# Convolution stages spread through the attention, and the maximum pass traced earlier

## The chip, the cores and the metric

The kernel runs on one core of a Trainium2 chip. The metric is the device time of one execution in microseconds, as the median of several runs. TensorE (PE) multiplies matrices, VectorE (DVE), ScalarE (ACT) and GpSimd (POOL) do the rest, and SyncE (SP) issues most DMAs. Each engine takes its instructions in order from its own queue and waits on semaphores.

## What is computed

The reference is one layer of a hybrid encoder over 2048 tokens of width 1024, in float32. Cut to what matters here:

```python
proj = u @ w_in
a  = mla_group(q part, kv part)          # 8 heads: softmax(q k^T * scale) v over 2048 keys
hy = hyena_group(conv part, filters)     # two orders; 512 channels
#   for o in 0, 1:  y = irfft(rfft(z, 4096) * filt_f[o])[:2048];  z = gate[o] * (y + z * bias[o])
mixed = concat(rms_norm(a), rms_norm(hy)) @ w_o
x = layer_norm(alpha * x + gate * mixed)
...                                      # then 16 routed experts, each choosing 256 tokens
```

The attention and the two long convolutions need only the projections. They don't depend on each other until `w_o` joins them.

## The kernel before

The program is traced in Python. A planner then puts each engine's instructions in order: it runs down the program on a simulated clock and gives a free engine the earliest traced instruction that is ready by that clock. So the traced order is a priority, and the order in which the chip works is fixed before it runs.

**The attention** (`attention`, L771) takes 32 blocks, each of one head and 512 queries. A block `n` has 16 inner steps `k` of 128 keys each. A step makes the scores in a PSUM bank `s` with three matmuls (L866 to L868: high and low halves of the numbers), takes two exponentials of them on ScalarE (`eh` L874 and the full one L875), the low half `el` on VectorE (L65), adds `eh` to the row sums `acc` on POOL (L881), and two steps later multiplies with the values (`pv`, L859 and L860, into the banks `o` and `l`). The exponentials need each query's maximum. It is found a block ahead: 16 times `max_step` (L798), a matmul into a bank `x` and a reduction on VectorE (L805). Then `max_row` (L807) takes the maximum of four parts, copies it into column 96 of `mz` (L811), transposes `mz` on TensorE (L814) and writes the row into the queries (L815), where the next block's first score reads it. `max_row` is traced at step 14. `close_block` (L825) ends the block before at step 3, and stores its output from SP's queue (L837).

**The convolutions** (`hyena`, L631) are a generator that works through stages of each order `o`, on channel halves `i`: `spectrum` (8 tasks), `fwd1` (8 tasks, the first transform), the middle stages `first_half` and `second_half` (16 tasks of each: transform, product with the spectrum on VectorE, ScalarE and POOL, transform back), and `inv` (8 tasks). Between stages the data goes through DRAM (Ad, F_dr, Bd, Z1). A task issues its loads and its stores itself, all from SP's queue, in the order in which they are traced. All its matmuls use one PSUM bank, `h` (`psH`, L931). Loads land in the tags `ta` (three buffers), `tb` and `tc` (two each).

**Side by side.** `beside` (L917) first makes values and keys of the later heads, then runs `hyena`. `drive` (L945 and L946) takes 1.5 of its steps for each of the first 12 steps of the attention, and 0.7 for each later one; what is left comes behind the attention (L947). Then `w_o` follows (weights from L984 on, output of the attention and the convolutions from L991 on).

Of the kernel before, what the change touches and what calls it, by code (L numbers as in the profile page):

```python
# [48 lines left out]
def hybrid_layer(ctx, tc, I, out):  # L49
# [581 lines left out]
    def hyena(hp, hw, bk):  # L631
# [7 lines left out]

        def fwd1(o, i, q4):  # L640
            hc = slice(i * HC, (i + 1) * HC)
            w1c = hw.tile([128, 4, 256], F32, name="ta", bufs=3)
            SY.dma_start(w1c, I["k_w1c"][:, q4 * 1024:q4 * 1024 + 1024].rearrange("p (q m) -> p q m", q=4))
            zt = hw.tile([128, 4, HC], F32, name="tb")
            SY.dma_start(zt, ZS[o][:, q4 * 4:q4 * 4 + 4, hc])
            for q2 in range(2):
                ev = hw.tile([128, 2, 2, HC], F32, name="tc")
                for qq in range(2):
                    ql = q2 * 2 + qq
                    p = bk("h")  # L650
                    for mt in range(2):
                        T.matmul(p[:, mt * HC:(mt + 1) * HC], w1c[:, ql, mt * 128:mt * 128 + 128], zt[:, ql, :],
                                 start=True, stop=True)
                    A.activation(ev[:, :, qq, :], p.rearrange("p (m c) -> p m c", m=2), AF.Copy)
                    if qq == 0:
                        yield
                for mt in range(2):
                    q0 = q4 * 4 + q2 * 2
                    SY.dma_start(Ad[2 * o + i][mt * 128:mt * 128 + 128, q0:q0 + 2, :], ev[:, mt])
                yield  # L660

        def spectrum(o, g4):
            kt = hw.tile([128, 4, CH], F32, name="tc")
            SY.dma_start(kt, pat(Af[o], g4 * 4 * 128 * CH, [[CH, 128], [128 * CH, 4], [1, CH]]))
            for g2 in range(2):
                ev = hw.tile([128, 2, CH], F32, name="ta", bufs=3)
                for gg in range(2):
                    p = bk("h")
                    T.matmul(p, g2m[:, 1 if g4 + g2 + gg == 0 else 0, :], kt[:, g2 * 2 + gg, :], start=True, stop=True)  # L669
                    A.activation(ev[:, gg, :], p, AF.Copy)  # L670
                    if gg == 0:
                        yield
                g0 = g4 * 4 + g2 * 2
                SY.dma_start(F_dr[o][g0:g0 + 2].rearrange("g p c -> p g c"), ev)
                yield

        def first_half(o, i, g4):
            hc = slice(i * HC, (i + 1) * HC)
            kt = hw.tile([128, 4, HC], F32, name="ta", bufs=3)
            SY.dma_start(kt, pat(Ad[2 * o + i], g4 * 4 * 128 * HC, [[HC, 128], [128 * HC, 4], [1, HC]]))  # L680
            ff = hw.tile([128, 4, 2, HC], F32, name="tc")
            for hh in range(2):
                SY.dma_start(ff[hh * 64:hh * 64 + 64], pat(F_dr[o], g4 * 4 * 128 * CH + i * HC,
                                                           [[CH, 64], [128 * CH, 4], [64 * CH, 2], [1, HC]]))
            ys = YS[g4] = []
            for g2 in range(2):
                gs = slice(g2 * 2, g2 * 2 + 2)
                p = bk("h")
                for gg in range(2):
                    gi = g2 * 2 + gg  # L690
                    T.matmul(p[:, gg * HC:(gg + 1) * HC], zm[:, 2 if g4 + gi == 0 else 0, :], kt[:, gi, :],
                             start=True, stop=True)
                pv = p.rearrange("p (g c) -> p g c", g=2)
                pr = hw.tile([128, 2, HC], F32, name="pr")
                V.tensor_tensor(pr, pv, ff[:, gs, 0], OP.mult)
                zs = hw.tile([128, 2, HC], F32, name="zs")
                A.activation(zs[0:64], pv[64:128], AF.Copy, scale=-1.0)
                A.activation(zs[64:128], pv[0:64], AF.Copy)
                yield
                if g4 + g2 == 0:  # L700
                    p = bk("h")
                    T.matmul(p[:, 0:HC], zm[:, 3, :], kt[:, 0, :], start=True, stop=True)
                    A.activation(zs[:, 0], p[:, 0:HC], AF.Copy)
                G.tensor_tensor(zs, zs, ff[:, gs, 1], OP.mult)
                y = hw.tile([128, 2, HC], F32, name="y", bufs=4)
                G.tensor_tensor(y, pr, zs, OP.add)
                ys += [y[:, 0], y[:, 1]]

        def second_half(o, i, g4):
            bt = hw.tile([128, 4, HC], F32, name="tb")  # L710
            ys = YS.pop(g4)
            for g2 in range(2):
                pi = bk("h")
                for gg in range(2):
                    gi = g2 * 2 + gg
                    T.matmul(pi[:, gg * HC:(gg + 1) * HC], ivm[:, 1 if g4 == 0 and gi == 0 else 0, :], ys[gi],  # L716
                             start=True, stop=True)
                A.activation(bt[:, g2 * 2:g2 * 2 + 2, :], pi.rearrange("p (g c) -> p g c", g=2), AF.Copy)
                yield
            SY.dma_start(pat(Bd[2 * o + i], g4 * 4 * 128 * HC, [[HC, 128], [128 * HC, 4], [1, HC]]), bt)  # L720

        def inv(o, i, q4):
# [4 lines left out]
            gt = hw.tile([128, 4, HC], F32, name="tb")  # L727
            SY.dma_start(gt, HZ[1 + o][:, qs, hc])
            for q2 in range(2):
                b2 = hw.tile([128, 2, 2, HC], F32, name="tc")  # L730
                q0 = q4 * 4 + q2 * 2
                SY.dma_start(b2, Bd[2 * o + i][:, q0:q0 + 2, :].rearrange("(k p) q c -> p k q c", k=2))
                p = bk("h")
                for qq in range(2):
                    for kt in range(2):
                        T.matmul(p[:, qq * HC:(qq + 1) * HC], w2i[:, q2 * 2 + qq, kt, :], b2[:, kt, qq, :],
                                 start=kt == 0, stop=kt == 1)
                q_ = slice(q2 * 2, q2 * 2 + 2)
                V.tensor_tensor(gt[:, q_], p.rearrange("p (q c) -> p q c", q=2), gt[:, q_], OP.mult)
                if q2 == 0:  # L740
                    yield
            SY.dma_start(ZO[o][:, qs, hc], gt)

        YS = {}

        def turns(*gens):
            gens = list(gens)
            while gens:
                for g in list(gens):
                    if next(g, gens) is gens:  # L750
                        gens.remove(g)
                    else:
                        yield

        for o in range(2):
            for g4 in range(8):
                yield from spectrum(o, g4)
            for i in range(2):
                for q4 in range(4):
                    yield from fwd1(o, i, q4)  # L760
            for i in range(2):
                yield from first_half(o, i, 0)
                for g4 in range(1, 9):
                    yield from turns(second_half(o, i, g4 - 1), *([first_half(o, i, g4)] if g4 < 8 else []))
            for i in range(2):
                for q4 in range(4):
                    yield from inv(o, i, q4)
                    yield
# [927 lines left out]
```

## Time and profile before

| | us |
|---|---|
| median of 3 runs | 3455.32 (3454.94 to 3457.93) |
| the profiled execution | 3456.35 |
| its span in the trace | 3454.6 |
| blocks of the attention, first score to last close | 661 to 1872 |
| first dense matmuls of the next stage | about 1957 |
| mean granted TensorE clock | 0.958 of full speed |

All rows below come from one profiled execution. Times are microseconds unless marked ns. Busy time of TensorE is the time in which at least one matmul was under way. "PEclk" is the granted clock as a share of 2.4 GHz. A line such as `A <- B: 29.9, 15, 5.3` says that A's engine stood idle before A until B came: 29.9 us in total, 15 times, 5.3 at the longest.

### The profile page before, as it was taken

How to read it: one execution, taken by the hardware profiler on the slowest of the kernel's cores; microseconds unless marked ns; L12 is line 12 of the kernel's file. 1: busy time of each engine (PE TensorE's matmuls, PEld its weight loads, DVE VectorE, ACT ScalarE, POOL GpSimd, SP SyncE). 2: the span in 40 equal slices, each digit the busy share in tenths (PEclk: the TensorE clock that was granted, in tenths of full speed). 3: DMA queues.
4: the chain of work that ended last, by engine and by line, in shares of the span. 5: the costliest groups of instructions: out<-in, count | busy, mean ns of one | idle time of the engine just before them, and what ended most of it. 6: DMA issues, size and time to landing. Idle time of an engine off the chain costs nothing.

```text
span 3454.6 us, 41964 instructions
## 1 busy us (share of the span) xinstructions
PE 3196.6 (93%) x14790; PEld 2477.7 (72%) x14790; DVE 2301.5 (67%) x3528; ACT 1697.8 (49%) x2569; POOL 1456.5 (42%) x1134
## 2 busy tenths in 40 slices
PE   7899999899989999999998699599999999999897
PEld 3667787666767776677776488477788877887676
DVE  7975343776677776667774377776656566565886
ACT  4762222566667664667774244233444344444442
POOL 5750000556678784658886266300100010000564
PEclk9999999699999999999999899799999999999998
DMA  6444353356466467647456643455666566665784
GB/s 192 158 150 118 111 145 94 97 175 175 156 162 150 108 160 236 176 165 163 119 126 194 222 155 131 150 171 186 215 199 203 183 217 210 208 203 186 268 279 160
DMA packets 373755, 594.16 MB, mean 172 GB/s; under 512 B 36859, under 2 KB 190013, under 8 KB 373097
## 3 DMA queue, kind: packets, MB, share of 16 engines
q1 hardware_dynamic: 347097, 528.95, 48.5%
q0 software_dynamic: 26304, 62.00, 7.1%
q8 instruction: 117, 1.92, 0.2%
q14 instruction: 93, 0.76, 0.1%
q10 hardware_dynamic: 144, 0.52, 0.0%
HBM read 438.84 MB, written 152.58 MB: 171 GB/s over the span
## 4 chain that ended last, share of the span: by engine, by line
PE 70%; DVE 11%; DMA 8%; issue 4%; POOL 3%; ACT 3%; SPq 0%; POOLq 0%; DVEq 0%; ACTq 0%
PE g L73 9%; PE g L74 9%; PE g L75 8%; PE s L866 3%; PE s L867 3%; PE s L868 3%; PE o L859 3%; PE l L860 3%; PE x L803 3%; PE mm L75 3%; PE mm L74 3%; PE mm L73 3%; DMA w<-in_w_ada_dram 3%; PE h L669 2%; PE h L716 1%
## 5 line engine op out<-in xcount | busy, mean ns | idle before, releaser
L881 POOL TENSOR_TENSOR acc<-acc,eh 128x512 f32<-128x512 f32 x480 | 615.8, 1283 | 157.3 <-ACT eh L874 132.3
L65 DVE TENSOR_TENSOR wl<-raw,wh 128x2048 fp32r<-128x2048 f32 (+1 forms) x210 | 473.3, 2256 | 225.0 <-ACT wh L59 224.0
L59 ACT ACTIVATE wh<-raw 128x2048 fp32r<-128x2048 f32 x192 | 367.5, 1915 | 439.9 <-PE g L75 341.4
L65 DVE TENSOR_TENSOR el<-s,eh 128x512 fp32r<-128x512 f32 x512 | 349.2, 687 | 158.2 <-ACT s L875 153.2
L805 DVE TENSOR_REDUCE mx<-x 128x1 f32<-128x512 f32 x512 | 346.4, 685 | 140.5 <-PE x L803 138.1
L73 PE MATMUL g<-wh,xh 128*128 128x512 f32 x1024 | 411.1, 402 | 3.2 <-DVE xh L62 2.3
L74 PE MATMUL g<-wl,xh 128*128 128x512 f32 x1024 | 408.3, 399 | 1.6 <-DVE wl L65 1.5
L75 PE MATMUL g<-wh,xl 128*128 128x512 f32 x1024 | 407.5, 398 | 1.0 <-DVE xl L65 1.0
L874 ACT ACTIVATE eh<-s 128x512 fp32r<-128x512 f32 x512 | 304.9, 596 | 205.1 <-PE s L868 179.0
L1495 POOL DMA_INDIRECT ACC<-ye,idx x30 | 65.8, 2195 | 691.0 <-DVE ye L1486 565.5
L875 ACT ACTIVATE s<-s 128x512 f32<-128x512 f32 x512 | 304.5, 595 | 0.0
L860 PE MATMUL l<-el,vt 128*66 128x512 f32 x512 | 226.5, 446 | 0.6 <-DVE acc L820 0.4
L73 PEld LDWEIGHTS g<-wh,xh 128*128 128x128 f32 x1024 | 193.0, 188 | 47.0 <-DVE xh L62 3.1
L74 PEld LDWEIGHTS g<-wl,xh 128*128 128x128 f32 x1024 | 193.1, 189 | 45.4 <-DVE wl L65 2.7
L75 PEld LDWEIGHTS g<-wh,xl 128*128 128x128 f32 x1024 | 192.7, 188 | 45.7 <-DVE xl L65 1.8
L803 PE MATMUL x<-kh,qt 96*128 96x512 f32 x512 | 221.9, 446 | 1.8 <-DVE mx L805 1.6
L866 PE MATMUL s<-qt,kh 97*128 97x512 f32 x512 | 214.9, 420 | 3.3 <-ACT qt L815 2.7
L73 PE MATMUL mm<-uT,wh 128*128 128x512 f32 x512 | 207.8, 407 | 5.4 <-DVE uT L62 5.4
L73 PE MATMUL g<-wh,hh 128*128 128x512 f32 x512 | 205.9, 403 | 5.8 <-ACT hh L59 5.8
L74 PE MATMUL g<-wl,hh 128*128 128x512 f32 x512 | 205.9, 402 | 5.2 <-DVE wl L65 5.2
L867 PE MATMUL s<-qt,kh 96*128 96x512 f32 x512 | 208.2, 407 | 0.0
L868 PE MATMUL s<-qt,kh 96*128 96x512 f32 x512 | 207.2, 405 | 0.0
(408 smaller groups left out, 6988.9 us busy)
## 6 DMA issues: line engine op xcount, KB each, us to landing
raw<-in_w_gate_dram SPq DMA_DIRECT2D x64, 1024.0 KB, 5.0
raw<-in_w_up_dram SPq DMA_DIRECT2D x64, 1024.0 KB, 7.1
raw<-in_w_down_dram SPq DMA_DIRECT2D x64, 1024.0 KB, 10.1
tc<-F_dr SPq DMA_DIRECT2D x64, 512.0 KB, 5.2
w<-in_w_ada_dram SPq DMA_DIRECT2D x48, 512.0 KB, 4.4
Af<-ev SPq DMA_DIRECT2D x32, 512.0 KB, 2.6
tc<-Af SPq DMA_DIRECT2D x16, 1024.0 KB, 6.4
F_dr<-ta SPq DMA_DIRECT2D x32, 512.0 KB, 3.0
```

Of the source, the lines that this page charges most:

```text
L59: return A.activation(hi, src, AF.Copy)
L65: return eng.tensor_tensor(lo, src, hi.bitcast(F32), OP.subtract)
L73: first = T.matmul(o, wh, xh, start=start, stop=False)
L74: T.matmul(o, wh, xl, start=False, stop=False)
L75: T.matmul(o, wl, xh, start=False, stop=stop)
L803: T.matmul(p, qh[0:96, i * 128:i * 128 + 128], khs[h % 2][0:96, 0, c * 512:c * 512 + 512], start=True, stop=True)
L805: V.tensor_reduce(mx[:, i, c:c + 1], p, axis=AX.X, op=OP.max)
L860: T.matmul(pl[0:66], vt[:, k, 64:130], el, start=k == 0, stop=k == NT - 1)
L866: T.matmul(p, kh[0:97, ks], qh[0:97, :], start=True, stop=False)
L867: T.matmul(p, kh[0:96, ks], ql[0:96, :], start=False, stop=False)
L868: T.matmul(p, kl[0:96, ks], qh[0:96, :], start=False, stop=True)
L881: G.tensor_tensor(acc, acc, eh.bitcast(F32), OP.add)
```

## The change

The convolutions' stages become a list of tasks. Each task first issues its loads and then gives control back. The runner starts the loads of the next task when the present one has done its first piece, and at that point also issues the stores of the task before, which are kept in the list `stores`. `first_half` and `second_half` become one task `mid`, which does the first half of group `g4` and the second half of group `g4 - 1`, taking turns. `spread` puts the nine `mid` tasks of one order and channel half among tasks of other stages, at even distances: spectrum, first transform and inverse of the other halves and orders. `inv` loads its data in one DMA of twice the size, and `fwd1` stores in two larger DMAs instead of four. `tb` gets a third buffer.

In the attention, `max_step` is traced behind the step's exponentials, with a priority 60 instructions higher; all 16 are done by step 12, and there `max_row` and `set_row` (its transposes and the write into the queries) are traced, at the same raised priority. The products of a block's last two steps are traced in steps 0 and 1 of the next block, and the first product of a block in step 3. The block before is closed at step 5, and its output is stored at step 7 (`keep`). Heads are loaded at step 3. `mz` has 98 columns instead of 128. The attention's steps give the convolutions 1.5 steps each for the first 12 and 0.8 after that, none at steps 5 and 9.

```diff
         def fwd1(o, i, q4):
...
-            zt = hw.tile([128, 4, HC], F32, name="tb")
+            zt = hw.tile([128, 4, HC], F32, name="tb", bufs=3)
             SY.dma_start(zt, ZS[o][:, q4 * 4:q4 * 4 + 4, hc])
...
+            yield
+            ev = hw.tile([128, 2, 4, HC], F32, name="tc")
+            for ql in range(4):
+                p = bk("h")
                 for mt in range(2):
...
+                A.activation(ev[:, :, ql, :], p.rearrange("p (m c) -> p m c", m=2), AF.Copy)
                 yield
+            for mt in range(2):
+                stores.append((Ad[2 * o + i][mt * 128:mt * 128 + 128, q4 * 4:q4 * 4 + 4, :], ev[:, mt]))
...
-        def first_half(o, i, g4):
+        def mid(o, i, g4):
             hc = slice(i * HC, (i + 1) * HC)
...
+            yield
+            done = YS.pop((i, g4 - 1), None)
...
             for g2 in range(2):
...
+                    G.tensor_tensor(y, pr, zs, OP.add)
+                    ys += [y[:, 0], y[:, 1]]
+                    yield
+                if done:
+                    pi = bk("h")
...
+                    A.activation(bt[:, g2 * 2:g2 * 2 + 2, :], pi.rearrange("p (g c) -> p g c", g=2), AF.Copy)
+                    yield
+            if done:
+                stores.append((pat(Bd[2 * o + i], (g4 - 1) * 4 * 128 * HC, [[HC, 128], [128 * HC, 4], [1, HC]]), bt))
...
+        def spread(mids, others, lead):
+            mids, others = list(mids), list(others)
+            for k in range(lead):
+                yield mids[k]
+            n = len(mids) - lead
+            for k in range(n - 1):
+                yield from others[k * len(others) // (n - 1):(k + 1) * len(others) // (n - 1)]
+                yield mids[lead + k]
+            yield mids[-1]
...
+        nine = range(9)
+        tasks = [*group(fwd1, 0, 0), *group(spectrum, 0),
+                 *spread(group(mid, 0, 0, n=nine), group(spectrum, 0, n=range(4, 8)) + group(fwd1, 0, 1), 1),
+                 *spread(group(mid, 0, 1, n=nine), group(inv, 0, 0) + group(fwd1, 1, 0) + group(spectrum, 1), 2),
+                 *spread(group(mid, 1, 0, n=nine), group(spectrum, 1, n=range(4, 8)) + group(inv, 0, 1)
+                         + group(fwd1, 1, 1), 2),
+                 *spread(group(mid, 1, 1, n=nine), group(inv, 1, 0, n=range(2)), 2),
+                 *group(inv, 1, 0, n=range(2, 4)), *group(inv, 1, 1)]
+        next(tasks[0])
+        for n, t in enumerate(tasks):
+            late, stores[:] = list(stores), []
+            for k, _ in enumerate(t):
+                if k == 0:
+                    for d, src in late:
+                        SY.dma_start(d, src)
+                    if n + 1 < len(tasks):
+                        next(tasks[n + 1])
+                yield
...
-        mz = kp.tile([128, 4, 128], F32, name="mz")
+        mz = kp.tile([128, 4, 98], F32, name="mz")
...
             V.tensor_copy(mz[:, :, 96], nm.bitcast(F32))
+
+        def set_row(n):
+            qh = blk[n][0]
             p = bk("x")
             for i in range(4):
-                T.transpose(p[:, i * 128:i * 128 + 128], mz[:, i, :], ident)
+                T.transpose(p[0:98, i * 128:i * 128 + 128], mz[:, i, :], ident)
             A.activation(qh[96:97, :], p[96:97, :], AF.Copy)
...
                 A.activation(eh, p, AF.Exp, scale=SCALE)
                 A.activation(p, p, AF.Exp, scale=SCALE)
+                with tc.high_priority(offset=60):
+                    for j in itertools.islice(maxes, 2 if k in (2, 6, 11) else 1):
+                        max_step(n + 1, j)
                 lo_of(V, el, p, eh)
...
-                if k >= 2:
-                    pv(k - 2)
-                if k == 3 and pend is not None:
-                    close_block(pend[0], osb, pend[3])
+                for g in {0: (-2,), 1: (-1,), 2: (), 3: (0,), 4: (1, 2)}.get(k, (k - 2,)):
+                    if g >= 0 or n > 0:
+                        pv(n + g // 16, g % 16)
+                if n > 0:
+                    if k == 1:
+                        done[n - 1] = free_sums(*live.pop(n - 1), accs[n - 1])
+                    if k == 5:
+                        oo = close_block(n - 1, done.pop(n - 1), accs.pop(n - 1))
+                    if k == 7:
+                        keep(n - 1, oo)
+                if k == 3 and b == 0 and 0 < h < H - 1:
+                    load_head(h + 1)
                 if k == 9 and n + 2 < NB:
                     query(n + 2)
-                if k == 14 and n + 1 < NB:
-                    max_row(n + 1)
-                yield
...
+                if n + 1 < NB:
+                    if k == 12:
+                        with tc.high_priority(offset=60):
+                            max_row(n + 1)
+                            set_row(n + 1)
+                yield k not in (5, 9)
...
-        drive(itertools.islice(at, 12), hy, 1.5)
-        drive(at, hy, 0.7, -1.0)
+        credit = 0.0
+        for n, free in enumerate(at):
+            credit += free * (1.5 if n < 12 else 0.8)
+            while credit >= 1.0:
+                credit -= 1.0
+                next(hy, None)
         drive(hy)
```

## Rows read from the trace of the kernel before

**Rows 1.** The page, busy time of each engine over the whole span.
```profile
PE 3196.6 (93%) x14790; PEld 2477.7 (72%) x14790; DVE 2301.5 (67%) x3528; ACT 1697.8 (49%) x2569; POOL 1456.5 (42%) x1134
```

**Rows 2.** Busy by stretch: length, PE, PEld, DVE, ACT, POOL, PEclk, DMA share, GB/s.
```profile
980.00:1262.00 282.00, 257.46 (x1108) 201.07 (x1106) 215.71 (x334) 193.35 (x358) 241.98 (x198) 0.95 0.53 126
1580.00:1858.00 278.00, 260.59 (x1144) 204.23 (x1145) 204.46 (x334) 199.22 (x367) 243.73 (x200) 0.96 0.55 131
661.00:1872.00 1211.00, 1139.98 (x4863) 867.66 (x4862) 868.13 (x1393) 809.94 (x1504) 880.20 (x718) 0.97 0.57 157
1380.00:1540.00 160.00, 156.19 (x654) 113.76 (x653) 110.30 (x177) 110.16 (x206) 100.14 (x82) 1.00 0.55 168
1872.00:1957.00 85.00, 40.29 (x135) 28.71 (x135) 16.93 (x27) 8.55 (x12) 3.65 (x4) 0.76 0.84 285
```

**Rows 3.** Waits of PE from 661 to 1872: total us, times, longest.
```profile
PE x L814 <- DVE mz L811: 29.9, 15, 5.3
...
PE s L866 <- ACT qt L815: 2.7, 8, 0.6
```

**Rows 4.** Timeline: start, us, engine, line, operation [idle before, releaser].
```profile
990.94 4.78 DVE L811 COPY mz<-nm 128x4 f32<-128x4 f32 x1
...
994.44 1.25 POOL L704 TENSOR_TENSOR zs<-zs,tc 128x512 f32<-128x512 f32 x1
...
995.78 1.12 PE L814 MATMUL x<-ident,mz 128*128 128x128 f32 x4 [5.31 <-DVE mz L811]
```

**Rows 5.** Busy in the 12 us from 992, columns as in the second group.
```profile
992.00:1004.00 12.00, 7.97 (x21) 6.10 (x22) 8.36 (x8) 4.21 (x9) 7.67 (x8) 0.57 0.44 87
```

**Rows 6.** Timeline of VectorE, the two other long copies.
```profile
1145.09 3.57 DVE L811 COPY mz<-nm 128x4 f32<-128x4 f32 x1
...
1184.96 3.31 DVE L811 COPY mz<-nm 128x4 f32<-128x4 f32 x1
```

**Rows 7.** All copies of L811: ns shortest/median/longest, first and last start.
```profile
L811 DVE COPY mz<-nm x32: 152/208/4784, 656.8 to 1838.9; 128x4 f32<-128x4 f32 x32
```

**Rows 8.** The chain that ended last, in order of time: start, us, what.
```profile
1867.41 1.74 PE h L736 x8
1869.17 0.70 DVE tb L739
1869.92 1.99 PE h L736 x8
...
1872.88 8.44 DMA tc<-Bd
...
1932.75 0.50 SPq L978
...
1957.12 0.70 PE mm L73 x3
```

**Rows 9.** Waits of SP's queue from 755 to 1932, columns as for PE.
```profile
SPq L720 <- ACT tb L718: 239.1, 32, 12.4
...
SPq L837 <- DVE oo L835: 109.7, 28, 10.1
```

**Rows 10.** PE by stage: spectrum, middle and inverse of the first order.
```profile
755.00:862.00 107.00, 104.19 (x411) 1.00 0.64 191
...
972.00:1262.00 290.00, 265.46 (x1143) 0.95 0.54 128
1262.00:1356.00 94.00, 86.09 (x369) 0.95 0.81 238
```

**Rows 11.** Timeline of PE, two neighbouring products of the spectrum.
```profile
804.13 1.13 PE L669 MATMUL h<-tc,g2m 128*128 128x512 f32 x2 [0.23 <-ACT ta L670]
805.94 1.13 PE L669 MATMUL h<-tc,g2m 128*128 128x512 f32 x2 [0.69 <-ACT ta L670]
```

**Rows 12.** All reductions of L805: ns shortest/median/longest, first and last start.
```profile
L805 DVE TENSOR_REDUCE mx<-x x512: 657/684/694, 637.4 to 1837.0; 128x1 f32<-128x512 f32 x171
```

**Rows 13.** DMA issues: count, KB each, median us from issue to landing.
```profile
at<-AO SPq DMA_DIRECT2D x16, 256.0 KB, 3.3
...
AO<-oo SPq DMA_DIRECT2D x31, 128.0 KB, 2.0
```

More of the change, by code (lines that the diff above doesn't have):

```diff
@@ L670, in spectrum @@
                     A.activation(ev[:, gg, :], p, AF.Copy)
[L671 to L672 removed]
+                    yield
                 g0 = g4 * 4 + g2 * 2
[L674 to L677 removed]
+                stores.append((F_dr[o][g0:g0 + 2].rearrange("g p c -> p g c"), ev))
+        def mid(o, i, g4):
             hc = slice(i * HC, (i + 1) * HC)
[L679 to L685, printed above, removed]
[L686 to L707 removed]
@@ L709, in second_half @@
[L709 to L720, printed above, removed]
+            if g4 < 8:
+                kt = hw.tile([128, 4, HC], F32, name="ta", bufs=3)
+                SY.dma_start(kt, pat(Ad[2 * o + i], g4 * 4 * 128 * HC, [[HC, 128], [128 * HC, 4], [1, HC]]))
+                ff = hw.tile([128, 4, 2, HC], F32, name="tc")
+                for hh in range(2):
+                    SY.dma_start(ff[hh * 64:hh * 64 + 64], pat(F_dr[o], g4 * 4 * 128 * CH + i * HC,
+                                                               [[CH, 64], [128 * CH, 4], [64 * CH, 2], [1, HC]]))
@@ L722, in inv @@
+            if done:
+                stores.append((pat(Bd[2 * o + i], (g4 - 1) * 4 * 128 * HC, [[HC, 128], [128 * HC, 4], [1, HC]]), bt))
         def inv(o, i, q4):
@@ L742, in inv @@
[L742 to L768, printed above, removed]
+                yield
@@ new lines, in inv, with group @@
+            stores.append((ZO[o][:, qs, hc], gt))
+        YS, stores = {}, []
+        def spread(mids, others, lead):
[7 more added lines that the diff above has]
+            yield mids[-1]
+        def group(f, *a, n=range(4)):
+            return [f(*a, k) for k in n]
@@ L771, in attention @@
+        next(tasks[0])
[7 more added lines that the diff above has]
+                        next(tasks[n + 1])
+                yield
+        for d, src in stores:
+            SY.dma_start(d, src)
+        yield
     def attention(kp, aw, bk):
-        mz = kp.tile([128, 4, 128], F32, name="mz")
+        mz = kp.tile([128, 4, 98], F32, name="mz")
@@ L836, in close_block, with keep @@
                             rc[:, :, None].to_broadcast([128, 4, 64]), OP.mult)
+            return oo
+        def keep(n, oo):
+            h, b = divmod(n, 4)
             (G if n == NB - 1 else SY).dma_start(AO[:, b * 4:b * 4 + 4, h * 64:h * 64 + 64], oo)
@@ L843, in attention, with pv @@
             max_step(0, j)
[L844 removed]
+            yield 1
         max_row(0)
[L846 removed]
+        set_row(0)
+        live, done = {}, {}
+        def pv(n, k):
+            if k == 0:
+                live[n] = bk("o"), bk("l")
+            po, pl = live[n]
+            eh, el = ph.pop((n, k))
+            vt = vts[n // 4 % 2]
+            T.matmul(po, vt[:, k, 0:128], eh, start=k == 0, stop=k == NT - 1)
+            T.matmul(pl[0:66], vt[:, k, 64:130], el, start=k == 0, stop=k == NT - 1)
+        ph, accs = {}, {}
         for n in range(NB):
             h, b = divmod(n, 4)
[L849 to L850 removed]
             qh, ql, _ = blk[n]
[L852 to L862 removed]
+            kh, kl = khs[h % 2][:, 0], khs[h % 2][:, 1]
+            acc = accs[n] = aw.tile([128, 512], F32, name="acc")
+            maxes = iter(range(16 if n + 1 < NB else 0))
             for k in range(NT):
```

86 lines of the change are left out of this document (41 added, 45 removed).

## The prediction

> **What bounds the kernel now.** I read the page first: TensorE is busy for 93% of the span, VectorE for 67%, POOL for 42% [rows 1]. So time can only be won where TensorE idles or runs at its lower clock, and the next view, the busy time by stage, shows where [rows 2]. From 661 to 1872 us, when the 32 blocks of the attention run, TensorE is busy for 1140.0 of 1211 us at a mean granted clock of 0.97: 71 us are idle, and 0.03 x 1211 = 36 us go to the lower of the two clock levels (1.2 instead of 2.4 GHz). Part of the 36 falls into idle time; I charge 30 to busy time, so the work at full clock is 1140 - 30 = 1110 us and the stage loses 101. The loss isn't even. From 1380 to 1540, beside the spectrum and the first transform, TensorE is busy for 156.19 of 160 us at clock 1.00 (0.976). From 980 to 1262 and from 1580 to 1858, beside the middle stages, it is busy for 518 of 560 us at 0.95 and 0.96, and there POOL is busy for 242 of 282 and 244 of 278 us. Behind the blocks come 85 us in which TensorE is busy for 40.3, at clock 0.76.
>
> The third view, TensorE's waits, names the largest single wait: 29.9 us for the copy of the row of maxima, and 2.7 us for that row's way into the queries [rows 3]. The timeline of one such place explains it [rows 4]. The copy of 128x4 numbers took 4.78 us, from 990.94 to 995.72, and POOL's operation that ran at its end closed at 995.69. TensorE's transposes stood behind the copy and waited 5.31 us. In the 12 us from 992 on TensorE was busy for 7.97 at a mean clock of 0.57 [rows 5], some 4.5 us of work, so this place cost 7.5. Two more copies took over 3 us [rows 6]; the median of all 32 is 0.208 and the shortest 0.152 [rows 7].
>
> Last I read what comes after the blocks: the chain of work runs through the convolutions' loads (8.44 us for one) and their matmuls, and only at 1932.75 does SP come to the next stage's loads, whose matmuls run dense from about 1957 [rows 8]. The convolutions are late, though the order in which they are traced puts their end into block 26 (318 steps; 18 in the first 12 of the attention's 529 steps, then 0.7 for each). They are a chain of their own: one PSUM bank (h=1), two buffers for most loads, and an SP queue that works in order and stands at stores whose data isn't there, 239.1 us at the Bd stores, 109.7 at the attention's output [rows 9]. The next loads are queued behind them.
>
> **The change part by part.** (1) *Loads one task ahead, stores one task late, `keep` two steps late.* SP's waits at stores lie off TensorE's path, but on the convolutions'. From 755 to 1932 us the convolutions take 1177 us, among them 107 for 8 spectrum tasks, 290 for 16 middle tasks, 94 for 8 inverse tasks in the first order [rows 10]. A spectrum step costs 107/32 = 3.3 us; where its load is there, bank to bank is 1.81 us (804.13 to 805.94) [rows 11]: 64 steps x 1.5 = 96 us to win. An inverse task costs 94/8 = 11.8 us, two halves of 5.9; where nothing is waited for, a half is 2.5 us (1867.41 to 1869.92) [rows 8], and with a step's queueing on TensorE and VectorE perhaps 3.3: 32 halves x 2.6 = 83 us to win. To end with the blocks (about 1840, below) the convolutions need 1177 - (1840 - 755) = 92 us less, half of the 179 on offer, so I take it that they do; the other end is rival B. Fewer, larger DMAs (32 instead of 64 Ad stores, 16 instead of 32 Bd loads) save SP 48 issues; nothing waits for those, so nought, and if SP were the bound, 48 x 0.50 us [rows 8] = 24.
>
> (2) *Middle stages spread.* There are 36 pieces among the other tasks instead of two rows of 16, with the same matmuls. POOL's work is moved, not reduced: 880 of 1211 us over the stage, 73%, where it is 86 to 88% in the middle stages and 63% (100 of 160) in the clean stretch now [rows 2]. At 1180 us it would be 75% throughout. A piece's second half uses products made a piece earlier, so TensorE need not wait for POOL there. The steps become 351, against 18 + 3.2 + 0.8 x 14 x 32 = 380 offered, so the trace ends in block 29; the pace for each inner step, 0.8 x 14/16 = 0.7, stays.
>
> (3) *Maximum pass earlier.* The copy and the transposes are traced at k = 12 instead of 14, and 60 instructions ahead of that. An inner step lasts 1211/512 = 2.4 us, so the row has some three steps more before the next block's first score needs it. The 32.6 us [rows 3] are the most this can give directly; the least is below nothing, since the transposes too are traced early and stand in order on TensorE: if the copy meets a busy POOL, all matmuls behind them wait. I take two thirds as won, nearest to the median copy of 0.208 us. What covers its cost: a maximum (median 0.68 us [rows 12]) now goes ahead of `el` on VectorE, and `pv`, which needs `el`, comes two or three steps, some 5 us, later; so nought, and 0.68 x 512 = 350 us if that slack were gone.
>
> (4) *The rest.* `mz` with 98 instead of 128 columns, the products of a block's last two steps traced in the next block, head loads at k = 3 on the same POOL queue, a third buffer for `tb`: the same operations in the same number, nothing I can tell from nought.
>
> **The sum** goes against the profiled execution (span 3454.6, its time 3456.35; the median of the runs is 3455.32, so nothing is shifted). The work is 1110 plus the 20 us of inverse products that now stand behind the blocks (some 90 passes of 1.74/8 us [rows 8]) = 1130 us. TensorE gets 1110/1211 = 0.917 done per us now, and 0.976 in the clean stretch. I take two thirds of the way, 0.956, since the last third is waits that the change leaves (TensorE for ACT behind each product of the convolutions, and some three blocks at the end with no other work beside them): 1130/0.956 = 1182, so the blocks end at 661 + 1182 = 1843. From there to dense matmuls it takes at most the 25 us from the convolutions' end to 1957 that the trace has now, at least the 2.0 and 3.3 us of the output's store and load [rows 13] and about as much again for what computes around them, some 12; I take 18: 1861. That is 96 us earlier than 1957. 3456 - 96 = **3360 us**.
>
> **The rivals.** *A, the forecast:* the blocks run near the clean stretch and the convolutions end with them. With 0.976 and a handover of 12 us: 661 + 1158 + 12 = 1831, so 3330; this is the low end.
>
> *B, the convolutions still end last.* They stay a chain on one bank; a middle task costs 290/16 = 18 us now [rows 10], and I found nothing that shortens its inside for certain. If they win only 32 of the 92 us, they end at 1900, and with 25 us of handover the next stage is dense at 1925: 3424. For it: they are late in every phase now. Against it: the waits at stores go.
>
> *C, slower: the stall of the row of maxima goes into all blocks.* Place: the copy on VectorE, with TensorE's transposes early behind it. Price: the 7.5 us above. The stage loses 101 us now; with the 85 us behind the blocks cut to 18 and 20 us of work moved in, the break-even is 1957 - 18 - 661 - 1130 = 148 us lost. If every second block meets a full run of POOL (16 x 7.5 = 120), the others the 2.0 us that the 15 waits have on average (32), and the 38 us of other idle time (71 - 32.6) stay, 190 are lost: 3456 + 42 = 3498. It decides from about one block in three. Now it is three in 32, all where POOL is at 86% or more; spread, POOL is at 75%, but in every block.
>
> The Trainium skill, page "SBUF — State Buffer", section "SBUF: two separate sides", has a rule behind this: VectorE in its two-port mode and a POOL operation take the same port pair as an exclusive lock, held for the whole operation. By that rule a higher priority buys the copy nothing, and POOL work in every block makes the encounter more frequent: the sum would be C's or D's. The trace agrees that the copy ended with POOL's operation (995.72 and 995.69); its median of 0.208 us shows that most copies met no lock.
>
> *D, no change: the whole stage runs as the middle stages do now.* Work there is 518 less 21 us for the clock, 497 of 560, 0.888 per us: 1130/0.888 = 1273, end at 1934, with 18 us 1952: 3451. This is also the case in which the priority doesn't do what it says, because the planner that orders the queues goes by its own clock.
>
> **How the numbers follow.** A 0.66, B 0.17, D 0.06, C 0.11. A measurement of this kernel tells 0.2% (7 us) from no change; A and B are faster, D within, C slower: 0.83, 0.06, 0.11. The range runs from A's low end, 3330, to B, 3425, and leaves C and D out.
>
> **What would show it.** (1): the last inverse product ahead of the attention's last store, SP's first load of the next stage by then issued, SP's waits at the Bd stores below a quarter. (2): POOL between 70 and 80% in every stretch, TensorE at 0.96 or more with clock 0.99. (3): TensorE's wait at the transposes below 11 us, no copy above 1 us. The forecast is wrong if inverse products still end the chain (B), or if copies of several microseconds stand in blocks all along, with TensorE's transposes behind them and the clock down after each (C).

## The result and the profile after

| | before | after |
|---|---|---|
| median, us | 3456.62 (4 runs, 3454.94 to 3458.72) | 3412.74 (4 runs, 3407.28 to 3418.22) |
| ratio, 95% interval | | 0.9873 [0.9855, 0.9891] |
| the profiled execution, us | 3456.35 | 3418.22 |
| last matmul with the values (end of the blocks) | 1870 | 1832 |
| last matmul of the convolutions | 1932 | 1894 |
| next stage's matmuls dense from | 1957 | 1919.5 |

The change wins 44 us in the median, 38 in the profiled executions; 96 were forecast. All three marks move by the same 38 us: the blocks are shorter, and what stands behind them is as long as before.

The page's busy times, which answer [rows 1]:

```profile
PE 3182.5 (93%) x14790; PEld 2464.2 (72%) x14790; DVE 2286.1 (67%) x3528; ACT 1697.4 (50%) x2569; POOL 1456.0 (43%) x1134
```

TensorE is busy for 14 us less with the same 14790 matmuls, and the mean granted clock is 0.964 instead of 0.958: fewer of them ran at the lower clock. Busy time by stretch of the changed kernel, columns as in [rows 2]:

```profile
661.00:1829.00 1168.00, 1116.86 (x4824) 848.67 (x4823) 848.98 (x1385) 803.54 (x1495) 868.94 (x707) 0.99 0.59 161
980.00:1262.00 282.00, 265.87 (x1177) 206.98 (x1176) 203.01 (x329) 186.97 (x345) 209.92 (x172) 0.99 0.61 165
1380.00:1540.00 160.00, 156.22 (x676) 116.50 (x676) 119.69 (x195) 112.70 (x211) 127.49 (x105) 1.00 0.64 171
1580.00:1829.00 249.00, 239.36 (x1063) 188.03 (x1062) 180.94 (x295) 175.71 (x328) 200.59 (x165) 0.98 0.53 141
1829.00:1912.00 83.00, 43.72 (x147) 30.20 (x145) 15.60 (x24) 7.70 (x14) 14.61 (x15) 0.76 0.83 282
```

The clock is 0.98 to 1.00 in every stretch beside the attention (0.95 and 0.96 in two of them before), and POOL's share is 74, 80 and 81% instead of 86, 63 and 88% [rows 2]. The last line is the old tail again: 83 us at clock 0.76. TensorE's largest waits from 661 to 1829 (columns as in [rows 3]), and then all copies of the row of maxima (as in [rows 7]):

```profile
PE x L829 <- DVE mz L823: 14.8, 13, 3.0
PE h L715 <- ACT zs L701: 6.8, 6, 2.7
```

```profile
L823 DVE COPY mz<-nm x32: 152/270/1328, 657.0 to 1800.2; 128x4 f32<-128x4 f32 x32
```

The wait at the transposes is halved, and the longest copy takes 1.33 us instead of 4.78. What follows the blocks, from the chain that ended last (start, us, what), answers [rows 8]:

```profile
1828.88 1.73 PE h L736 x8
...
1855.95 3.79 PE h L736 x8
1859.77 0.70 DVE tb L741
1860.52 3.79 PE h L736 x8
...
1869.92 7.75 DMA HY<-tb
1877.68 8.02 DMA tb<-HZ
...
1892.12 2.01 PE h L736 x8
...
1895.32 0.46 SPq L1011
1895.83 6.43 DMA raw<-in_w_o_dram
1902.27 9.63 DMA at<-AO
...
1919.55 0.70 PE mm L73 x3
```

Inverse products run until 1894, the chain passes through the DMAs of the last tasks (8.02 us for one), and SP comes to the next stage's first load at 1895.32. Eight matmuls that take 1.73 us beside the attention take 3.79 at 1855.95 and 1860.52, where the granted clock is 0.50, the lower level. This is rival B. SP's waits, columns as in [rows 9]:

```profile
SPq L856 <- DVE oo L850: 117.3, 26, 13.5
SPq L774 <- ACT ta L668: 86.1, 26, 7.9
SPq L774 <- ACT tc L654: 77.2, 15, 12.6
SPq L774 <- ACT tb L717: 66.9, 25, 5.9
```

All stores are now issued at L774. Those to Bd (`tb`) wait 66.9 us, down from 239.1 [rows 9]; that is 0.28 of it, where the prediction asked for less than a quarter. The stores to F_dr (`ta`) and Ad (`tc`) had these waits in the kernel before:

```profile
SPq L674 <- ACT ta L670: 114.8, 32, 11.2
...
SPq L659 <- ACT tc L654: 77.0, 23, 8.6
```

So SP stands at the convolutions' stores for 230 us instead of 431, and their end, measured from the blocks' end, hasn't moved.

**How many matmuls stand where.** Tile `h` is the convolutions' bank, so the busy time of its instructions counts their matmuls (in the first brackets, behind TensorE's busy time; PEld, VectorE and ScalarE follow). First the kernel before: tile `h` up to the blocks' end and from there to the convolutions' end, and then all instructions of the first stretch. Then the same three of the kernel after:

```profile
760.00:1870.00 1110.00, 314.50 (x1057) 199.43 (x1055) 57.02 (x83) 191.72 (x324) 0.97 0.59 158
1870.00:1932.00 62.00, 34.81 (x104) 24.22 (x104) 8.66 (x13) 0.00 (x0) 0.81 0.81 267
760.00:1870.00 1110.00, 1045.23 (x4471) 795.60 (x4469) 788.58 (x1262) 741.02 (x1373) 817.93 (x667) 0.97 0.59 158
```

```profile
761.00:1832.00 1071.00, 307.57 (x1041) 195.42 (x1042) 56.21 (x82) 187.10 (x316) 0.99 0.61 164
1832.00:1894.00 62.00, 39.45 (x120) 26.38 (x119) 8.97 (x13) 4.75 (x8) 0.78 0.84 282
761.00:1832.00 1071.00, 1025.77 (x4435) 780.66 (x4436) 767.48 (x1251) 731.42 (x1355) 804.89 (x657) 0.99 0.61 164
```

Before, (4471 - 1057)/1057 = 3.23 attention matmuls go by for each one of the convolutions; after, 3394/1041 = 3.26. The order is fixed before the run, so this ratio decides how many of the convolutions' 1161 matmuls are left when the blocks end: 104 before, 120 after. In this order the tail stays, however fast the blocks become. That became the theory, called "turn" below: **a product of the convolutions waits for its turn in TensorE's queue, not for its load.** Three rows of the kernel after, from the timelines of TensorE and ScalarE, show one step of the spectrum:

```profile
886.60 1.02 PE L667 MATMUL h<-tc,g2m 128*128 128x512 f32 x2
...
890.25 1.02 PE L667 MATMUL h<-tc,g2m 128*128 128x512 f32 x2
...
887.66 0.60 ACT L668 ACTIVATE ta<-h 128x512 f32<-128x512 f32 x1
```

ScalarE has emptied the bank at 888.26. The next product stands behind eight more attention matmuls and starts at 890.25, with no wait. The step is 3.65 us, with twelve attention matmuls in it. The kernel before has the same step:

```profile
779.51 1.02 PE L669 MATMUL h<-tc,g2m 128*128 128x512 f32 x2
...
783.16 1.02 PE L669 MATMUL h<-tc,g2m 128*128 128x512 f32 x2
```

Over all steps of the spectrum the median is 3.67 us in both kernels, with twelve attention matmuls between two products. The 1.81 us from bank to bank [rows 11] is a place where none stands between them; it says nothing about loads.

### The profile page after: what moved, and what is told of

Its sections match the earlier page's. It is cut to its first block, busy times and chain, and to the rows that moved or that the text cites. A ratio compares the mean times of both kernels' runs of the same rounds, so it can differ in the third digit from the quotient of the medians.

```text
span 3416.4 us, 41836 instructions
## 1 busy us (share of the span) xinstructions
PE 3182.5 (93%) x14790; PEld 2464.2 (72%) x14790; DVE 2286.1 (67%) x3528; ACT 1697.4 (50%) x2569; POOL 1456.0 (43%) x1134
## 4 chain that ended last, share of the span: by engine, by line
PE 69%; DVE 7%; DMA 6%; issue 3%; POOL 3%; ACT 3%; SPq 0%; POOLq 0%; DVEq 0%; ACTq 0%
PE g L73 9%; PE g L74 9%; PE g L75 9%; PE s L887 3%; PE s L888 3%; PE s L889 3%; PE x L815 3%; PE o L874 3%; PE l L875 3%; PE mm L75 3%; PE mm L74 3%; PE mm L73 3%; DMA w<-in_w_ada_dram 2%; PE h L667 2%; PE h L652 2%
## 5 line engine op out<-in xcount | busy, mean ns | idle before, releaser
L59 ACT ACTIVATE wh<-raw 128x2048 fp32r<-128x2048 f32 x192 | 367.5, 1915 | 440.4 <-PE g L75 329.4
L73 PE MATMUL mm<-uT,wh 128*128 128x512 f32 x512 | 208.2, 408 | 5.6 <-DVE uT L62 5.6
L887 PE MATMUL s<-qt,kh 97*128 97x512 f32 x512 | 206.3, 403 | 1.0 <-DVE el L65 1.0
L74 PE MATMUL mm<-uT,wh 128*128 128x512 f32 x512 | 206.4, 403 | 0.4 <-DVE uT L65 0.2
L75 PE MATMUL mm<-uT,wl 128*128 128x512 f32 x512 | 205.7, 402 | 0.0
```

Of the source, the lines that this page charges most:

```text
L59: return A.activation(hi, src, AF.Copy)
L73: first = T.matmul(o, wh, xh, start=start, stop=False)
L74: T.matmul(o, wh, xl, start=False, stop=False)
L75: T.matmul(o, wl, xh, start=False, stop=stop)
L887: T.matmul(p, kh[0:97, ks], qh[0:97, :], start=True, stop=False)
```

## The experiments

"Matmuls behind" are those of the convolutions behind the blocks' last one; "ratio in the order" is that of attention to convolutions while both run, worked out as above. Kernels with the same time of before beside them ran together on one chip.

| kernel | time, us | before beside it | ratio, 95% interval | convolutions end | blocks end | ratio in the order | matmuls behind |
|---|---|---|---|---|---|---|---|
| before | | | 1 | 1932 | 1870 | 3.23 | 104 |
| after | 3412.74 | 3456.62 | 0.9873 [0.9855, 0.9891] | 1894 | 1832 | 3.26 | 120 |
| e2_attention_only | 3460.45 | 3452.36 | 1.0025 [1.0010, 1.0040] | 1946 | 1888 | 3.16 | 88 |
| e4_two_h | 3422.69 | 3452.36 | 0.9926 [0.9904, 0.9948] | 1502 | 1908 | 1.70 | 0 |
| e5_two_s | 3345.66 | 3452.36 | 0.9709 [0.9683, 0.9736] | 1817 | 1840 | 2.87 | 0 |
| e1b_tasks_only | 3434.36 | 3449.67 | 0.9957 [0.9939, 0.9974] | 1915 | 1873 | 3.18 | 88 |
| e7_no_ahead | 3415.05 | 3449.67 | 0.9902 [0.9873, 0.9932] | 1895 | 1834 | 3.26 | 120 |
| e6_act_copy | 3384.98 | 3449.67 | 0.9822 [0.9796, 0.9848] | 1864 | 1834 | 3.10 | 64 |
| e9_before_two_s | 3383.22 | 3449.67 | 0.9809 [0.9781, 0.9836] | 1860 | 1865 | 2.93 | 0 |
| e10_two_s_act | 3331.49 | 3449.66 | 0.9648 [0.9626, 0.9669] | 1810 | 1827 | 2.88 | 0 |
| e8_tasks_two_s | 3337.20 | 3449.66 | 0.9672 [0.9652, 0.9692] | 1808 | 1831 | 2.88 | 0 |
| c4_two_s_noahead | 3369.98 | 3449.66 | 0.9762 [0.9741, 0.9783] | 1845 | 1859 | 2.90 | 0 |
| e13_before_two_s_act | 3348.71 | 3449.66 | 0.9706 [0.9685, 0.9726] | 1825 | 1832 | 2.92 | 0 |
| e14_tasks_two_s_act | 3327.42 | 3457.91 | 0.9637 [0.9606, 0.9667] | 1789 | 1819 | 2.86 | 0 |
| c1_x1_h2 | 3797.33 | 3457.91 | 1.0994 [1.0949, 1.1039] | 1431 | 2291 | 1.13 | 0 |

**The two parts alone.** e2_attention_only has the new `attention` and the runner's new pace, with the old `hyena`. e1b_tasks_only has the new `hyena` and the 98 columns of `mz`, with the old attention and the old pace.

> The new attention (maximum pass earlier and with raised priority, new closing) beside the old convolutions, whose stores are issued at once and whose middle stages stand in two rows. Theory 'even load': POOL is still busy for 86% in the middle stages, the copies still take up to 5 us there, the waits at the transposes stay at 25 us or more: 3445 to 3455. Theory 'priority': the waits fall below 15 us in total: about 3430.

> The new convolution tasks beside the old attention: maximum row at step 14, no raised priority, old closing of blocks, steps offered at 0.7 for each inner step (mz has the 98 columns that the memory needs). Theory 'even load': the stalls of the row of maxima went because POOL's work is even now, so most of the 40 us by which the blocks end earlier comes with the tasks alone; the copies stay below 1.5 us and the waits at the transposes below 18 us, the time is about 3425. Theory 'priority': the earlier row is what took the stalls away; the waits stay near 30 us: about 3445.

Measured: 1.0025 and 0.9957; their product is 0.998, and together they give 0.9873. TensorE's wait at the transposes in the first, then in the second:

```profile
PE x L817 <- DVE mz L811: 33.9, 13, 4.7
```

```profile
PE x L826 <- DVE mz L823: 23.7, 14, 5.4
```

Tracing the row of maxima earlier is no help while POOL has its full stretches (33.9 us against 29.9 [rows 3]), and spreading POOL's work alone brings the wait to 23.7; both leave the blocks' end at 1873 or later, with the clock at 0.97 up to there. So neither theory holds alone: e2_attention_only fits "even load" in its waits, e1b_tasks_only lies between the two. Only together do the blocks end at 1832.

**Loads in the task's own turn** (e7_no_ahead): the changed kernel without the loads ahead; the stores still go a task late.

```diff
-        next(tasks[0])
-        for n, t in enumerate(tasks):
+        for t in tasks:
             late, stores[:] = list(stores), []
+            next(t)
...
-                    if n + 1 < len(tasks):
-                        next(tasks[n + 1])
```

> The changed kernel without its early loads: each task issues its loads when its turn comes; stores stay one task late. Theory 'loads' (step 1 of the prediction: what the convolutions wait for is loads, 96 us of the spectrum and 83 of the inverse): the convolutions end 60 us or more later and the time goes above 3450. Theory 'order on TensorE' (the bank is free for 1.4 us before each product because attention matmuls stand ahead of it in TensorE's queue, whether the data is there or not): they end within 20 us of the changed kernel's, and the time is 3400 to 3435.

Measured 0.9902 against 0.9873 for the changed kernel: some 10 us at most, and the intervals overlap. The convolutions end at 1895, as with the loads ahead. So, with three score banks, waiting for loads was not what made them late, and the first step of the prediction falls.

**One score bank less** (e5_two_s), **that bank given to the convolutions** (e4_two_h), and **one less in the kernel before** (e9_before_two_s):

```diff
-        at_ = Banks(st, "psT", s=3, x=2, o=1, l=1)
-        hb_ = Banks(st, "psH", h=1)
+        at_ = Banks(st, "psT", s=2, x=2, o=1, l=1)
+        hb_ = Banks(st, "psH", h=1)     # e5_two_s, e9_before_two_s; h=2 in e4_two_h
```

> The changed kernel with two instead of three banks for the scores and still one for the convolutions: the price of the bank that the kernel with two convolution banks takes away. Theory 'one bank': the attention is a little slower and the convolutions keep the pace of their chain, so that the blocks end some 30 to 60 us later, nearer to the convolutions' end at about 1895, and the whole is within 15 us of the changed kernel, 3400 to 3425. Theory 'loads': the same, since the loads are the same; this kernel tells nothing between the two and is the control.

> The changed kernel with two banks for the convolutions' products and two instead of three for the scores. Theory 'one bank': the convolutions end last because each of their products waits for the reader of the one before; with two banks they end with the blocks, the 87 us behind the blocks shrink to some 25, and the 25 us of work there move in: 3412 - 87 + 25 + 25 = 3375, if two banks for the scores cost TensorE nothing; with a price of 0.03 of the stage 3410. Theory 'loads': the convolutions are held by their loads and stores; they end as late as now, above 3410.

> The kernel before with two instead of three banks for the scores. Theory 'order on TensorE': a third bank of scores lets the attention go ahead of the convolutions in TensorE's queue; with two the convolutions come sooner here too, end with the blocks, and most of the 85 us behind the blocks goes; the middle stages keep their stalls: about 3415. Rival 'the tasks are needed': without loads ahead and stores behind, the convolutions still end last; within 15 us of 3455.

Measured: 0.9709, 0.9926 and 0.9809. None of the three expectations saw it: e5_two_s was to be within 15 us of the changed kernel and is some 57 us faster by the ratios (0.9709 against 0.9873), e9_before_two_s was to win some 40 us and wins 66, and in e4_two_h the convolutions end far earlier than either theory had it. With two score banks the ratio in the order falls to 2.87 and 2.93; as I read it, fewer attention matmuls are ready by the planner's clock while the convolutions' bank is being emptied. The convolutions then end before the blocks in both kernels, and in e5_two_s the next stage's matmuls are dense from 1853, 13 us behind the blocks' end instead of 87. The blocks themselves end about where they did, though all of the convolutions' work now lies beside them. The stretch from 1829 to 1912 in e5_two_s:

```profile
1829.00:1912.00 83.00, 77.90 (x392) 62.19 (x393) 56.30 (x97) 45.80 (x83) 54.26 (x42) 0.94 0.50 172
```

TensorE is busy for 77.9 of 83 us where the changed kernel has 43.7. This one number, in the kernel *before*, is worth more than the whole change. e4_two_h shows the other side: with a second bank the convolutions are through at 1502 at a ratio of 1.70, and 400 us of attention follow without them. The Trainium skill, page "Perfetto Trace Analysis", section "Matmul Optimizations", asks to see to it that all eight PSUM banks are used; here the kernels that leave one of the eight empty are faster by 1.7 and 1.9% than those that use it.

**Which bank it is** (c1_x1_h2): three score banks kept, two for the convolutions, one for the maxima.

```diff
-        at_ = Banks(st, "psT", s=3, x=2, o=1, l=1)
-        hb_ = Banks(st, "psH", h=1)
+        at_ = Banks(st, "psT", s=3, x=1, o=1, l=1)
+        hb_ = Banks(st, "psH", h=2)
```

> The changed kernel with its eight PSUM banks dealt otherwise: three for the scores as in the changed kernel, one instead of two for the maxima, two instead of one for the convolutions. It asks whether the third score bank itself holds the convolutions back, or their single bank. Theory 'turn' (with one bank a product can only be put into TensorE's order where the planner's clock has the bank free, and every attention matmul that is ready goes ahead of it): with a second bank the product is ready early, the 3.2 attention passes for each pass of the convolutions fall to nearly 1, the convolutions end near 1400 us, and the attention has 500 us for itself. Then TensorE has nothing to fill the attention's waits with, the blocks end at 1900 or later, and the time is no better than 0.99 of before. Rival, the third score bank itself: the convolutions end near 1890 as in the changed kernel.

Measured: the ratio in the order is 1.13 and the convolutions end at 1431. So a third score bank doesn't hold the convolutions back when they have two banks of their own. That their single bank lets the attention's ready matmuls go ahead, and that the number of score banks says how many are ready, fits all these kernels, but it isn't shown: c1_x1_h2 changes two banks at once, and the single bank for the maxima slows the attention too, so it may have a share in the 1.13, which no run separates. A faster pace of the trace changes nothing: planned with 1.2 instead of 0.8 steps for each inner step, the changed kernel has the same order on every engine. The time, 1.0994, is far above "no better than 0.99", and another bank is the reason. TensorE's largest wait and its busy time from 1431 to 2291, when the attention is alone, and then its busy time in e4_two_h, alone as well but with two banks for the maxima:

```profile
PE x L815 <- DVE mx L817: 104.2, 133, 2.2
```

```profile
1431.00:2291.00 860.00, 663.30 (x2333) 455.42 (x2331) 495.19 (x797) 386.88 (x715) 448.41 (x363) 0.79 0.11 21
1502.00:1908.00 406.00, 386.25 (x1610) 266.13 (x1608) 333.99 (x547) 262.78 (x494) 310.78 (x253) 0.98 0.17 37
```

With one bank for the maxima, 133 of the 304 matmuls of the next maximum in this stretch wait for the reduction before them, and TensorE is busy for 0.77 of it at a granted clock of 0.79. With two banks the attention alone keeps it busy for 0.95 at 0.98, so the missing convolutions aren't the reason.

**The copy on ScalarE** (e6_act_copy on the changed kernel, e10_two_s_act with two score banks as well, e13_before_two_s_act both on the kernel before):

```diff
-            V.tensor_copy(mz[:, :, 96], nm.bitcast(F32))
+            A.activation(mz[:, :, 96], nm.bitcast(F32), AF.Copy)
```

> The changed kernel with the copy of the row of maxima on ScalarE instead of VectorE. If POOL's running operations hold VectorE's copy, the copies are all of one length now (0.2 to 0.4 us), the 14.8 us of waits at the transposes fall below 6 and the waits behind them too: 3395 to 3405. If the waits come from the place of the transposes in TensorE's queue and not from POOL, they stay above 10 us: 3412 within 6.

> The changed kernel with two instead of three score banks and the copy of the row of maxima on ScalarE. Theory 'turn' (each product of the convolutions waits for its turn in TensorE's queue; one score bank less gives it an earlier turn): two banks alone gave 0.9709 of the kernel before, and the copy alone 0.9822 where the changed kernel had 0.9873, about 18 us. With two banks the convolutions end with the blocks already (1817 against 1840 us), so the copy can only give what its stalls cost the blocks: the wait at the transposes falls from 13.5 to under 3 us, and the time from 0.971 to about 0.967 of before, 3338 us. Rival: the gain of the copy in the changed kernel was won in its tail alone, by another order of the queues; then nothing is left to win here and the ratio stays at 0.971.

> The kernel before with the two small edits alone: two score banks, and the copy of the row of maxima on ScalarE. Two banks alone gave 0.9809, with 17.9 us of waits at the transposes and 8.1 us for the low halves. If those waits are the rest between it and the changed kernel with two banks (0.9709), this run comes to about 0.975. If the rest is the convolutions' longer chain of whole stages (ending at 1860 us instead of 1817), the ratio stays at 0.980 and the convolutions still end at about 1860.

Measured: 0.9822, 0.9648 and 0.9706. All copies of e6_act_copy, and what is left of the wait at the transposes:

```profile
L823 ACT ACTIVATE mz<-nm x32: 195/209/213, 656.0 to 1802.9; 128x4 f32<-128x4 f32 x32
```

```profile
PE x L829 <- ACT mz L823: 1.7, 2, 1.1
```

The same 128x4 numbers never take more than 0.213 us on ScalarE, where VectorE took up to 4.78 us beside POOL's operations [rows 4]. That long time is VectorE's alone. It agrees with the lock named in the prediction (the Trainium skill, page "SBUF — State Buffer", section "SBUF: two separate sides"), by which ScalarE never waits on the pair that VectorE and POOL share. In e6_act_copy the gain shows in the tail (64 matmuls behind instead of 120), since the order is another too. The time of e6_act_copy, 3385 us, is below the 3395 to 3405 expected. In e13_before_two_s_act it is more than either side expected: blocks and convolutions both end some 35 us earlier than in e9_before_two_s. Both stand in the one queue that the copy stalls; the wait at the transposes there was 17.9 us, the clock up to the blocks' end goes from 0.98 to 0.99, and what the rest was isn't shown. Two edited lines of the kernel before thus give 2.9%, against 1.3% for the change.

**What is left of the change then** (e8_tasks_two_s: the new tasks, the old attention, two score banks; e14_tasks_two_s_act: with the copy on ScalarE as well; c4_two_s_noahead: e5_two_s with the loads in the task's own turn):

> The new task list of the convolutions beside the attention as it was before the change, with two score banks. It asks what the attention part of the change is worth once the tail is gone. If the attention part has its worth in the blocks (row of maxima earlier, products handed over to the next block), this is slower than both parts with two banks (0.9709), near 0.978, with a wait at the transposes above 17 us. If its worth was only that it put fewer passes of the convolutions behind the last block, it has none here, and the ratio is within 0.002 of 0.971.

> The new task list of the convolutions, the attention as it was before the change, two score banks, and the copy of the row of maxima on ScalarE. Beside it stand 0.9672 (the same with the copy on VectorE) and 0.9648 (with the new attention as well). If the new attention is worth something in itself, this stays above 0.9648. If its worth was only that the row of maxima had more time for the copy's stalls, then with a copy of 0.2 us it has none: the wait at the transposes (11.6 us with VectorE's copy) goes, and the time comes to about 0.9672 less 10 us of 3450, 0.964, 3326 us.

> The changed kernel with two score banks, in which each task issues its loads in its own turn and not a task ahead (the stores still go one task late). With three banks this cost at most 10 us, since the products waited for their turn on TensorE and not for the loads. With two banks the products' turn comes sooner. Theory 'turn' with loads as the next limit: the loads' latency now shows, the convolutions end behind the last block, and the ratio goes from 0.971 to about 0.985. Rival: the loads are hidden by two or three buffers anyway; the ratio stays within 0.003 of 0.971 and the convolutions end before the last block.

Measured: 0.9672, 0.9637 and 0.9762. The attention's part brings nothing once the convolutions end in time: 0.9709 with it and 0.9672 without, 0.9648 and 0.9637 with the copy on ScalarE, the intervals of each pair overlapping. The tasks do: 0.9706 [0.9685, 0.9726] without them and 0.9637 [0.9606, 0.9667] with them. The loads ahead are worth 0.5% here (0.9762 against 0.9709), between the two expectations: where the turn comes sooner, loads do show, and the convolutions end at 1845 instead of 1817. TensorE waits 6.8 us for loads from Ad in c4_two_s_noahead, and not at all for them in e5_two_s. e14_tasks_two_s_act has the shortest time of the study, 3327 us, where its second expectation had it; e10_two_s_act can't be told from it, and e8_tasks_two_s hardly.

## Why the prediction was right and wrong

**Step (1) failed: the convolutions don't end with the blocks.** It read the spectrum's 3.3 us against 1.81 us from bank to bank [rows 10, 11] as waiting for loads, did the same with the inverse, put 179 us on offer and took 92 of them as won. But the steps of 1.81 and 2.5 us that it measured by have no attention matmul (the spectrum) or two (the inverse) between two products; the usual steps there, 3.67 and 5.69 us, have twelve and seventeen. The convolutions won 38 us, and those because the blocks became shorter. With loads in place a step still takes 3.65 us, most of it behind attention matmuls in the queue; without the loads ahead the end moves by less than 1 us (e7_no_ahead). Two views of the trace before would have told it. One is TensorE's waits at tile `h` from 755 to 1870, where a DMA is named twice:

```profile
PE h L669 <- DMA tc<-Af: 2.6, 1, 2.6
PE h L736 <- DMA tc<-Bd: 2.3, 1, 2.3
```

TensorE stood before a load of the convolutions for 4.9 us in all, against the 179 on offer. The other is the count of matmuls: 1161 x 3.23 = 3750 attention matmuls would have to stand beside the convolutions, and 3414 did.

**The handover** was taken as 18 us and is 87 (1832 to 1919.5), as before. That is 69 us, more than the 58 by which the profiled execution missed (38 won, 96 forecast); the other 11 are the blocks, which end at 1832 instead of 1843, with the 20 us of inverse products that were to move in still outside.

**Step (2) and the efficiency** were about right. I put the work at 1110 us, and at 0.956 of it per us without the inverse products it needs 1161 us; it took 1171 (661 to 1832), 0.948 per us. POOL's 74 to 81% answers "70 to 80%". TensorE is busy for 0.943, 0.976 and 0.961 of the three stretches, where 0.96 was asked of each.

**Step (3)** was taken as two thirds of 32.6 us; the wait at the transposes fell by 15.1 (29.9 to 14.8), about half, and the longest copy is 1.33 us where I asked for less than 1. Of the blocks' 38 us, from 661 to their last matmul with the values, 20 are idle time (71 to 51 us, the 15 among them) and 18 are busy time (1138 to 1120). Some 4 of the 18 are the 16 matmuls more that now stand behind the blocks; the other 14 go with the higher clock. But the cause isn't the one given there: with the old tasks the earlier row wins nothing (e2_attention_only). Why the two parts win only together is not settled. With two score banks the attention's part has no gain left, with the copy on VectorE as little as on ScalarE, so these runs don't say whether its worth lay in the copy's stalls or in the order; three score banks with ScalarE's copy and the old attention wasn't run.

**Step (4)**, the rest at nought: nothing in the runs speaks against it.

**The rivals.** B, with 0.17, is what came, though not as its text has it: its 3424 came from convolutions that gain 32 us in a chain of their own, and their end at 1894 (1900 there) came from the order. The 3413 us lie inside the range only because the range was drawn up to B. C did not come: no copy above 1.33 us, though long copies stand in other kernels (5.0 us in e5_two_s, 7.2 in e4_two_h). D didn't either, at 0.948 per us where it has 0.888.

## What to carry to other kernels

Where two streams share an engine's queue in an order fixed beforehand, count how many instructions of the one go by for each of the other: the ratio tells which stream is left over at the end. While a stream waits for its place, loads issued earlier gain next to nothing (e7_no_ahead); once its place comes sooner, they do (c4_two_s_noahead). The number of PSUM banks that each stream has moved this ratio in every kernel here, and one bank fewer for the stream that runs ahead can be worth more than a restructured one. An idle time belongs to the engine only where the row shows it idle; a long step on a busy engine is a place in the queue.

## What was not expected of the hardware

A copy of 128x4 numbers takes 0.195 to 0.213 us on ScalarE in all 32 cases of e6_act_copy, and between 0.152 and 4.78 us on VectorE in the kernel before [rows 7]. The longest of these, from 990.94 to 995.72, stood not through one of POOL's operations but through four; these three came ahead of the one in [rows 4]. A lock that is held for one operation explains this only if the copy is passed over between them, which no run shows directly.

```profile
990.78 1.25 POOL L881 TENSOR_TENSOR acc<-acc,eh 128x512 f32<-128x512 f32 x1
992.00 1.25 POOL L706 TENSOR_TENSOR y<-pr,zs 128x512 f32<-128x512 f32 x1
993.22 1.25 POOL L881 TENSOR_TENSOR acc<-acc,eh 128x512 f32<-128x512 f32 x1
```

And the granted clock can be low where all waits are short: in c1_x1_h2 no wait of TensorE from 1431 to 2291 is longer than 2.2 us, 197 of the 860 us are idle, and the mean clock is 0.79.
